# Attention projections as 512-column products handed out block by block inside the attention loop, and the operand copies of the attention issued from ScalarE's queue

## The chip, the cores and the metric

The kernel runs on one core of one Trainium2 chip. Its engines are PE (TensorE, with its weight loads shown apart as PEld), DVE (VectorE), ACT (ScalarE), POOL (GpSimd) and SP (SyncE, which here only issues transfers). The metric is the time of one execution on the device in microseconds; what counts is the median of several runs.

## The reference: one inference step of a two-layer trunk

Rows are 640 tokens of 1024 values: 512 of a new prompt and 8 running streams with 16 new tokens each. Layer 0 mixes with a gated MLP and a short convolution, layer 1 with attention over 16 heads of 64 with a learned decay, and each is followed by a convolutional feed-forward block. The change lies in the attention layer:

```python
def _fox_project(x, w_in, b_f, q_norm, k_norm):
    z = x @ w_in                                  # 1024 -> q, k, v of 1024 each, f of 16
    q, k, v, f = jnp.split(z, [D_C, 2 * D_C, 3 * D_C], axis=-1)
    q = _rmsnorm(q.reshape(b, t, C_HEADS, C_HEAD_DIM), q_norm)
    k = _rmsnorm(k.reshape(b, t, C_HEADS, C_HEAD_DIM), k_norm)
    ...
def _fox_attend(q, k, v, dq, dk, q_pos, k_pos):
    s = jnp.einsum('bthd,bshd->bhts', q, k) * (C_HEAD_DIM ** -0.5)
    s = s + dq - dk                               # cumulated log forget values
    s = jnp.where(k_pos <= q_pos, s, NEG_INF)
    return jnp.einsum('bhts,bshd->bthd', jax.nn.softmax(s), v)
```

The prompt attends to itself; the streams attend to a cache of 256 rows and to their own new rows. The result goes through the output projection `w_out` and is added to the residual. k, v, the forget values and the convolution states are outputs too.

## The kernel before

Every large product is made of three single-pass products of split values (high part times high, low times high, high times low), so a weight tile of 128x1024 is loaded as `raw` (512 KB, from SP), its high part `whi` is cast on ACT, and its low part `wlo` is `raw - whi`. `weights` (L83) makes the low part on DVE (L95); `weights_added` (L107) makes it as a negated copy on ACT (L103) and a transfer from POOL that adds the source on top (L104). There are five `whi`/`wlo` buffers and four of `raw`.

The instructions of each engine run in one fixed order. It is made when the program is built, by a scheduler that follows a model of the time: of the instructions that are ready, it takes the one that was written first. So the place of a call in the Python text is its priority, and what is written late fills the holes of what is written early.

The attention layer (from L935) works on four groups of four heads. For each group `project` (L678) computes q, k and v, 256 columns each: for every one of the five row blocks `tb` of 128 tokens (the fifth holds the streams) 24 products into half a PSUM bank `pj` (L701), eight row chunks `kc` of the weights times three. An eviction on ACT scales them into `z` (L704). For q and k, ACT squares (L709), DVE sums by head (L710) and scales (L300), POOL takes the power -1/2 (L301), and after the fifth row block DVE multiplies the whole tile by the result (L713), and k by its norm as well (L715). `decay` (L607, called after the first q) computes the forget values with 48 products `pf`, a scan, and a way through HBM: `s_b`, `s_d` and `s_n` are written and read back by SP.

Then the group's attention runs. `stream_operands` (L791) transposes the streams' q and k. `operands` (L723) transposes q and k of one pair of heads, and for each of the two heads makes four operand tiles `qa`, `ka`, `qb`, `kb`: two casts on ACT (L738, L741), two on DVE (L740, L743), and four transfers from SP (L739, L742, L745, L746). The four tiles have three buffers each. For each of two pairs a fixed list is walked: `"b30", "s0", "b31", "o", "b20", "s1", "b21", "b10", "b11", "b00", "b01"`. `b31` is the prompt's query block 3 of the pair's head 1, `s0` is a pair of streams, `o` makes the next pair's operands. `prompt_block` (L757) makes two score products (L763, L764), a softmax on DVE and ACT, transposes of the probabilities (L770), a copy (L773 or L775) and the products with v (L777, on a tile of 64 columns of weights). A score needs one of two PSUM banks `sc`.

After the four groups come the eight blocks `po` of the output projection over the first heads (L968 to L979), with products of 320 columns; what needs the last heads follows with the next stage (L993). By the priority above, the projections of group g+1 are what fills PE's holes in the attention of group g, and the blocks `po` fill those of group 3. When nothing of the attention is ready, PE takes one product of 256 columns, then looks again.

The change touches `weights_added`, `project`, `operands`, `prompt_block`, some buffer counts in `stream_operands` and `streams_pair`, the attention part of `build`, and the layout of the weights on the host.

## Time and profile before

| what | value |
|---|---|
| median of 3 runs (1505.16 to 1507.6) | 1505.55 us |
| the profiled execution, its whole time | 1503.4 us |
| its span, from the first instruction to the last | 1501.6 us |
| mean granted TensorE clock | 0.991 |
| HBM read, written | 147.43 MB, 11.54 MB |

The profile is of one execution. Its page gives busy time by engine, the span in 40 slices, the DMA queues, the chain of work that ended last and the costliest groups of instructions. On PE the duration of a matmul is longer than its turn, since matmuls overlap in the pipeline: the time that one takes out of PE's stream is the distance between the starts of neighbours, and the chain in order of time shows it, since there a run of matmuls is listed with the time to the next piece. "LDWEIGHTS" rows (PEld) run beside the matmuls. A row of the queue of an engine (SPq, ACTq) is an instruction that issues a transfer.

### The profile page before, as it was taken

To read this page: it belongs to the slowest core of one execution; us is meant where nothing else is said; L and a number is where in the kernel's file an instruction comes from. 1 tells how busy PE (TensorE), PEld (TensorE's weight loads), DVE (VectorE), ACT (ScalarE), POOL (GpSimd) and SP (SyncE) were. 2 spreads that over 40 slices of the span, in tenths; PEclk is the share of its full clock that TensorE was granted. 3 is DMA by queue.
4 is the path that set the end of the run, shared out by engine and by line. 5 is a ranking of instruction groups with operands and counts; after the bars stand their busy time and mean duration, and the time that the engine had idled before them with its cause. 6 is when DMAs were issued, how large, how long until landed. Compare 5 with 4: busy or idle time off the path is not lost.

```text
span 1501.6 us, 26356 instructions
## 1 busy us (share of the span) xinstructions
PE 1470.4 (98%) x10576; PEld 1417.9 (94%) x10576; DVE 1050.5 (70%) x1799; ACT 727.0 (48%) x1316; POOL 194.5 (13%) x229
## 2 busy tenths in 40 slices
PE   8999999899999999999999999999989999999998
PEld 6999999899999999999989888888979999999998
DVE  6555538977777777576676767768796776777764
ACT  5422325555555555445545454535455554555551
POOL 5100021201100010043111111003210000100000
PEclk9999999899999999999999999999989999999999
DMA  7222213444444444243534343522334433444432
GB/s 272 79 71 72 71 43 88 117 99 117 113 116 113 115 100 111 75 169 106 185 127 139 110 131 106 154 77 88 69 106 119 123 102 97 102 114 113 113 87 85
DMA packets 71786, 164.91 MB, mean 110 GB/s; under 512 B 13600, under 2 KB 21712, under 8 KB 71536
## 3 DMA queue, kind: packets, MB, share of 16 engines
q1 hardware_dynamic: 48304, 133.79, 28.2%
q0 software_dynamic: 10656, 22.02, 9.2%
q10 hardware_dynamic: 12704, 7.41, 1.7%
q8 instruction: 83, 1.36, 0.4%
q14 instruction: 39, 0.32, 0.1%
HBM read 147.43 MB, written 11.54 MB: 106 GB/s over the span
## 4 chain that ended last, share of the span: by engine, by line
PE 88%; DVE 6%; DMA 2%; ACT 2%; issue 2%; SPq 0%; ACTq 0%; DVEq 0%
PE mm L250 36%; PE zx L200 19%; PE pj L701 12%; PE aux L200 8%; PE pv L777 3%; PE po L250 3%; DMA wlo<-w_dn 2%; PE pt L770 1%; DVE hl L281 1%; DVE wlo L95 1%; PE mm L388 1%; PE pt L856 1%; PE sc L763 1%; PE sc L764 1%; DVE sl L136 1%
## 5 line engine op out<-in xcount | busy, mean ns | idle before, releaser
L135 ACT CAST sh<-raw 128x1024 fp32r<-128x1024 f32 (+2 forms) x152 | 142.8, 943 | 135.7 <-PE zx L200 87.0
L136 DVE TENSOR_TENSOR sl<-raw,sh 128x1024 fp32r<-128x1024 f32 (+2 forms) x152 | 165.0, 1092 | 55.4 <-ACT sh L135 55.2
L250 PE MATMUL mm<-sh,wlo 128*128 128x320 f32 x864 | 197.8, 310 | 3.2 <-DMA wlo<-w_dn 2.6
L250 PE MATMUL mm<-sh,whi 128*128 128x320 f32 x864 | 196.6, 310 | 0.6 <-ACT sh L135 0.6
L250 PE MATMUL mm<-sl,whi 128*128 128x320 f32 x864 | 197.0, 309 | 0.0
L200 PE MATMUL zx<-hl,sh 128*128 128x320 f32 x576 | 179.0, 311 | 2.1 <-DVE hl L136 2.0
L200 PE MATMUL zx<-hh,sh 128*128 128x320 f32 x576 | 178.0, 309 | 1.9 <-ACT sn L215 1.9
L200 PE MATMUL zx<-hh,sl 128*128 128x320 f32 x576 | 174.9, 309 | 0.0
L347 DVE SCALAR_TENSOR_TENSOR t<-zp,cst,t 128x656 f32<-128x656 f32 x184 | 163.8, 897 | 11.4 <-ACT t L345 10.3
L94 ACT CAST whi<-raw 128x1024 fp32r<-128x1024 f32 (+3 forms) x96 | 85.8, 896 | 148.9 <-PE mm L250 81.6
L250 PEld LDWEIGHTS mm<-sh,wlo 128*128 128x128 f32 x864 | 143.6, 188 | 5.9 <-DMA wlo<-w_dn 2.8
L358 DVE TENSOR_TENSOR x<-mm,x 128x640 f32<-128x640 f32 x103 | 84.5, 820 | 90.7 <-PE mm L250 90.4
L250 PEld LDWEIGHTS mm<-sh,whi 128*128 128x128 f32 x864 | 144.2, 188 | 1.9 <-ACT sh L135 1.1
L250 PEld LDWEIGHTS mm<-sl,whi 128*128 128x128 f32 x864 | 144.7, 188 | 0.2 <-DVE sl L136 0.2
L701 PE MATMUL pj<-whi,hl 128*128 128x256 f32 x480 | 137.9, 287 | 2.8 <-DVE hl L281 2.8
L701 PE MATMUL pj<-wlo,hh 128*128 128x256 f32 x480 | 137.6, 287 | 0.0
L701 PE MATMUL pj<-whi,hh 128*128 128x256 f32 x480 | 137.3, 287 | 0.0
L95 DVE TENSOR_TENSOR wlo<-raw,whi 128x1024 fp32r<-128x1024 f32 (+3 forms) x96 | 107.9, 1127 | 34.3 <-ACT whi L94 33.7
L250 PE MATMUL mm<-hl,whi 128*128 128x320 f32 x512 | 117.4, 310 | 2.0 <-DVE hl L281 2.0
L250 PE MATMUL mm<-hh,wlo 128*128 128x320 f32 x512 | 117.4, 311 | 0.4 <-DMA wlo<-w_up 0.4
L250 PE MATMUL mm<-hh,whi 128*128 128x320 f32 x512 | 117.7, 311 | 0.0
L200 PEld LDWEIGHTS zx<-hl,sh 128*128 128x128 f32 x576 | 108.4, 188 | 4.1 <-DVE hl L136 3.9
(232 smaller groups left out, 3341.5 us busy)
## 6 DMA issues: line engine op xcount, KB each, us to landing
raw<-w_up SPq DMA_DIRECT2D x88, 512.0 KB
raw<-w_dn SPq DMA_DIRECT2D x36, 512.0 KB
wlo<-w_dn POOLq DMA_DIRECT2D x36, 512.0 KB, 5.9
raw<-w_c SPq DMA_DIRECT2D x24, 512.0 KB
raw<-w_ab SPq DMA_DIRECT2D x16, 512.0 KB
ck<-c_k SPq DMA_DIRECT2D x16, 512.0 KB
cv<-c_v SPq DMA_DIRECT2D x16, 512.0 KB
o_kv<-z ACTq DMA_DIRECT2D x8, 640.0 KB
```

The source lines that it names most:

```text
L94: nc.scalar.copy(out=hi[:, c], in_=raw[:, c])
L95: nc.vector.tensor_tensor(out=lo[:, c], in0=raw[:, c], in1=hi[:, c].bitcast(F32), op=ALU.subtract)
L135: nc.scalar.copy(out=hi, in_=src)
L136: nc.vector.tensor_tensor(out=lo, in0=src, in1=hi.bitcast(F32), op=ALU.subtract)
L200: nc.tensor.matmul(out, lhsT=l[:, c], rhs=r, start=start and p == 0 and i == 0, stop=p == 3 and i == 2, skip_group_check=True)
L250: nc.tensor.matmul(outs[h], lhsT=l, rhs=r[:, h * HT:(h + 1) * HT], start=start and k == 0, stop=stop and k == 2)
L281: nc.vector.scalar_tensor_tensor(out=lo, in0=x, scalar=gs, in1=hi.bitcast(F32), op0=ALU.mult, op1=ALU.subtract)
L347: nc.vector.scalar_tensor_tensor(out=cv[:, 0:CW], in0=zp[:, i:i + CW], scalar=w[:, i:i + 1], in1=cv[:, 0:CW], op0=ALU.mult, op1=ALU.add)
L358: self.nc.vector.tensor_tensor(out=x, in0=ps[:, C0:C0 + T], in1=x, op=ALU.add)
L388: nc.tensor.matmul(pvs[tb], lhsT=l[:, tb * P:(tb + 1) * P], rhs=r[:, (kc % 2) * 512:(kc % 2 + 1) * 512], start=kc == 0 and k == 0, stop=kc ...
L701: nc.tensor.matmul(out[tb], lhsT=l[:, tb * P:(tb + 1) * P], rhs=r[:, c:c + 256], start=kc == 0 and i == 0, stop=kc == 7 and i == 2)
L777: nc.tensor.matmul(ov[64 * hh:64 * hh + 64, i * P:n], lhsT=z[2][:, j, (2 * pair + hh) * 64:(2 * pair + hh) * 64 + 64], rhs=u[:, j * P:(j + ...
```

## The change

`project` is replaced by two functions that return their output tiles and a list of five steps (three for the first call), one for each row block, to be called later. `project_qk` makes q and k of a group together, 512 columns wide; `project_v` makes v of two groups together, 512 wide. A step holds 24 products. The first step of a list loads its four weight tiles; for all but the first lists the first of the four is made with `weights_added`. The norm of q and k is finished in the last step of a list.

q and k of group 0, then `decay`, then v of groups 0 and 1 are done ahead of the attention. The other 20 steps (q and k of groups 1 and 2, v of groups 2 and 3, q and k of group 3) wait in a queue, and so do the eight output blocks in group 3. After chosen blocks of the list one step is taken from the queue; `issue_after` puts its instructions on PE behind the second score product of that block. The table `share` says how many for each group and pair, `after` which blocks. Since a step is now written behind its block, it comes ahead of the later blocks in priority. The output blocks take their weights from `weights_added`.

The four transfers of `operands` go from SP's queue to ACT's, in the loop over both heads. Buffers: the q/k tiles are 512 wide with two buffers (before: 256 wide, three), v has three (two), `sq` is 512 wide with one (256, two), `kts` and `on` one (two), `ckv` two (three).

```diff
-    def weights_added(self, src):
-        raw = self.raw()
+    def weights_added(self, src, cols=1024):
+        raw = self.raw()[:, 0:cols]
         self.nc.sync.dma_start(out=raw, in_=src)
-        return self.added(self.wp, ("whi", "wlo"), raw, src, 1024, 1024)
+        return self.added(self.wp, ("whi", "wlo"), raw, src, 1024, cols)
...
-    def project(self, g, h, first, after_q=None):
+    def walk(self, us, h, tbs, evict):
+        k, nc = self.k, self.nc
+        out = [self.pj.tile([P, 512], F32, tag="pj", name=k.nm("pj")) for _ in tbs]
+        for kc in range(8):
+            wh, wl = us[kc // 2]
+            hh, hl = h[kc]
+            c = (kc % 2) * 512
+            for tb, o in zip(tbs, out):
+                for i, (l, r) in enumerate(((hh, wh), (hl, wh), (hh, wl))):
+                    nc.tensor.matmul(o, lhsT=l[:, tb * P:(tb + 1) * P], rhs=r[:, c:c + 512],
+                                     start=kc == 0 and i == 0, stop=kc == 7 and i == 2)
+        for tb, o in zip(tbs, out):
+            evict(tb, o)
+
+    def project_qk(self, g, h, pairs=False):
...
+        zt = self.zp.tile([P, 5, 512], F32, tag="qk", name=k.nm("z"), bufs=2)
+        ss = self.zp.tile([P, 40], F32, tag="ss", name=k.nm("ss"))
+        def evict(tb, o):
+            nc.scalar.activation(out=zt[:, tb, :], in_=o, func=AF.Copy, scale=self.rt[:, tb:tb + 1])
+            sq = self.zp.tile([P, 512], F32, tag="sq", name=k.nm("sq"), bufs=1)
+            nc.scalar.activation(out=sq, in_=zt[:, tb, :], func=AF.Square)
+            s = ss[:, tb * 8:tb * 8 + 8]
+            nc.vector.reduce_sum(out=s, in_=sq.rearrange("p (h d) -> p h d", d=64), axis=AX.X)
+            k.rstd_of(s, s, 1.0 / 64)
+            if tb < 4:
+                return
+            zh = zt.rearrange("p t (h d) -> p (t h) d", d=64)
+            nc.vector.tensor_tensor(out=zh, in0=zh, in1=ss.unsqueeze(2).broadcast_to([P, 40, 64]), op=ALU.mult)
+            zk = zt[:, :, 256:512].rearrange("p t (h d) -> p t h d", d=64)
+            nc.vector.tensor_tensor(out=zk, in0=zk, in1=..., op=ALU.mult)
+            nc.scalar.dma_start(out=io["o_kv"][0, :, :, 256 * g:256 * g + 256]..., in_=zt[:, :, 256:512])
+        us = []
+        def step(tbs):
+            if not us:
+                us.extend((k.weights_added if g and u == 0 else k.weights)(io["w_qk"][g, u]) for u in range(4))
+            self.walk(us, h, tbs, evict)
+        walk = [(0, 1), (2, 3), (4,)] if pairs else [(tb,) for tb in range(5)]
+        return (zt[:, :, 0:256], zt[:, :, 256:512]), [lambda tbs=tbs: step(tbs) for tbs in walk]
+
+    def project_v(self, gg, h):
...
+        def evict(tb, o):
+            for i, zt in enumerate(zs):
+                nc.scalar.activation(out=zt[:, tb, :], in_=o[:, 256 * i:256 * i + 256], func=AF.Copy, scale=self.rt[:, tb:tb + 1])
...
@@ operands
-            nc.sync.dma_start(out=f(qa[b]), in_=f(qa[a]))
+            nc.scalar.dma_start(out=f(qa[b]), in_=f(qa[a]))
...
-            nc.sync.dma_start(out=f(kb[0:64]), in_=f(ka[a]))
+            nc.scalar.dma_start(out=f(kb[0:64]), in_=f(ka[a]))
...
-            nc.sync.dma_start(out=f(qb[64:68]), in_=io["s_b"][hd, 0:4])
-            nc.sync.dma_start(out=f(kb[64:68]), in_=io["s_b"][hd, 4:8])
+            nc.scalar.dma_start(out=f(qb[64:68]), in_=io["s_b"][hd, 0:4])
+            nc.scalar.dma_start(out=f(kb[64:68]), in_=io["s_b"][hd, 4:8])
@@ build
+    def out_block(ob):
+        n = cut[ob]
+        w = k.weights_added(io["w_oc"][ob, :, 0:n * P], n * P)
...
+    qk, steps = at.project_qk(0, h, True)
+    for f in steps:
+        f()
+    decay()
+    v, steps = at.project_v(0, h)
+    for f in steps:
+        f()
+
+    share = {(0, 0): 3, (0, 1): 4, (1, 0): 4, (1, 1): 4, (2, 0): 3, (2, 1): 2, (3, 0): 4, (3, 1): 4}
+    after = {2: ("b30", "b21"), 3: ("b30", "b31", "b21"), 4: ("b30", "b31", "b21", "b11")}
...
     for g in range(4):
-        z = at.project(g, h, g == 0, decay if g == 0 else None)
-        if g == 3:
+        z = qk + (v[g],)
+        if g == 0:
+            for i in (1, 2):
+                qks[i], steps = at.project_qk(i, h)
+                queue += steps
+            vs, steps = at.project_v(1, h)
+            v += vs
+            queue += steps
+        elif g == 1:
+            qks[3], steps = at.project_qk(3, h)
+            queue += steps
+        elif g == 3:
             o = [k.split(k.hp, HT_, at.o[c]) for c in range(6)]
+            queue += [lambda ob=ob: out_block(ob) for ob in (6, 7, 0, 1, 2, 3, 4, 5)]
...
-                    at.prompt_block(g, pair, int(st[2]), int(st[1]), z)
+                    score = at.prompt_block(g, pair, int(st[2]), int(st[1]), z)
+                    if st in after[share[g, pair]]:
+                        with tc.issue_after(score.ins):
+                            queue.pop(0)()
             at.prompt_end(g, pair)
...
+        qk = qks.get(g + 1)
```

91 lines of the change are left out of this document (35 added, 56 removed).

## The prediction

> **What bounds the kernel now.** I read the page first, then windows over the attention layer, then the chain in order of time for the turn of each kind of matmul. From the page:
>
> ```profile
> span 1501.6 us, 26356 instructions
> ...
> PE 1470.4 (98%) x10576; PEld 1417.9 (94%) x10576; DVE 1050.5 (70%) x1799; ACT 727.0 (48%) x1316; POOL 194.5 (13%) x229
> ...
> PE 88%; DVE 6%; DMA 2%; ACT 2%; issue 2%; SPq 0%; ACTq 0%; DVEq 0%
> ```
>
> PE bounds it: 88% of the chain that ended last. The windows show whether that also holds where the change is (columns: length, then busy time of PE, PEld, DVE, ACT, POOL, granted clock, DMA share, GB/s):
>
> ```profile
> 660.00:676.00 16.00, 13.18 (x103) 12.44 (x102) 12.16 (x17) 3.85 (x5) 7.23 (x12) 1.00 0.49 162
> 676.00:726.00 50.00, 50.00 (x411) 49.86 (x409) 29.80 (x55) 30.44 (x56) 12.99 (x13) 1.00 0.47 150
> 726.00:1016.00 290.00, 290.00 (x2630) 254.31 (x2629) 200.73 (x577) 134.84 (x351) 30.54 (x33) 1.00 0.39 123
> ```
>
> The first projection (660 to 726) leaves PE 2.8 us idle, the attention (726 to 1016) none. DVE is at 69% and ACT at 46% there, so neither binds over the whole stretch. A fuller PE can therefore bring nothing in the attention; only less work on PE can, and any hole that the new order leaves is a loss. How much of the 290 us is what, in counts, with the turns from the chain in order of time (start, time to the next piece, what):
>
> ```profile
> L701 PE MATMUL pj<-wlo,hh 128*128 128x256 f32 x337 | 97.2, 288 | 0.0
> L701 PE MATMUL pj<-whi,hl 128*128 128x256 f32 x336 | 97.0, 289 | 0.0
> L250 PE MATMUL po<-sl,whi 128*128 128x320 f32 x84 | 25.5, 317 | 0.0
> ```
>
> ```profile
> 702.17 14.39 PE pj L701 x120
> 31.83 2.72 PE mm L388 x12
> 1061.75 28.17 PE mm L250 x192
> ```
>
> The turn of a product of 256 columns is 14.39/120 = 0.120 us, of 320 columns 28.17/192 = 0.147, of 512 columns (in the first mixer, same kind of operands) 2.72/12 = 0.227. The 290 us hold 1009 projection products (337 + 2 x 336, the third kind has 336 too), 121 us, and 252 of `po` (3 x 84), 37 us. The other 132 us, 16.5 per pair of heads, are the attention's own.
>
> **The change, part by part.** *512 columns.* 1440 products of 0.120 (172.8 us) become 720 of 0.227 (163.4): 9.4 us less. The Trainium skill, "TensorE: Matmul & The Clock Gate", section "Wait — 56ns, not 53.3ns?", knows only some 2.5 ns beside the columns of a matmul; by that, 720 fewer would save 1.8 us. The three rows above speak for more: 64 columns from 256 to 320 cost 27 ns and 192 from 320 to 512 cost 80, so 0.42 ns each, and 0.120 less 256 of them leaves 13 ns per matmul. I take the rows.
>
> *Ahead of the attention.* The first score now comes at 725.94:
>
> ```profile
> 717.43 8.51 PE pj L701 x71
> 725.94 0.23 PE sc L763
> ...
> 684.16 2.06 PE pf L250 x14
> 686.22 1.11 PE pt L323 x10
> ```
>
> ```profile
> 714.77 0.25 SPq L745 DMA_DIRECT2D qb<-s_b  x1
> ```
>
> By then 431 projection products are done (1440 less 1009; of them the 120 and the 71 above), 51.7 us. After it, 240 of 512 columns must be, 54.4 us: that is 49 products of 256 more. With the 48 `pf` (7.1), the two small groups at L308 and L323 (about 2.3) and 12 transposes (1.3) I get 65.1 us from PE's start at 659.8, so 724.9. But the forget values are also needed: from the end of `pf` (686.2) to the first read of `s_b` (714.8) it takes 28.6 us. `pf` now stands behind all 120 products of q and k, in holes of their evictions or at their end: at about 696 instead of 686. That puts the read at 724.5 and the first score at about 727, 1.2 us later than now and with 5.9 us of projection (49 x 0.120) more behind it. Bounds: 0 later if `pf` goes into holes, 5 later if it comes whole behind q and k.
>
> *The fill of the attention.* 1009 products (121.1 us) become 20 steps of 24, 108.8 us: 12.3 us less between first score and end, the 5.9 and 6.4 from the width. Each pair has 16.5 us of its own and 3, 4, 4, 4, 3, 2 steps of 5.4, so 33, 38, 38, 38, 33 and 27 us; the last two have 120 and 132 products of `po`, 34 and 36. The steps come ahead of later blocks, so in the pairs with three or four PE has something to do until the last short blocks, and those are followed by the next pair's first score. I take 0.5 us of holes there in all (bounds 0 and 6).
>
> *A wait that is new.* In the last pair of group 2 only two steps are left, behind `b30` and `b21`, and the second ends q and k of group 3. Now `po` covers that place; then nothing may, since the output blocks stand behind the first score of group 3. From the end of that step to that score the path is one eviction, square, sum, scale, power, two multiplications, transposes, casts, a transfer. Rows for 256 columns, then the sum for 512 (L783), and PE's rows:
>
> ```profile
> L704 ACT ACTIVATE z<-pj,rt 128x256 f32<-128x256 f32 x43 | 18.6, 472 | 9.0 <-PE pj L701 8.7
> L709 ACT ACTIVATE sq<-z 128x256 f32<-128x256 f32 x28 | 11.2, 419 | 0.0
> L301 POOL TENSOR_TENSOR ss<-ss,mhalf 128x4 f32<-128x4 f32 x30 | 31.1, 1043 | 184.7 <-DVE ss L300 177.9 <-DVE l L786 6.6
> L783 DVE TENSOR_REDUCE m<-sc 128x1 f32<-128x512 f32 x12 | 8.2, 687 | 0.1
> L713 DVE TENSOR_TENSOR z<-z,ss 128x1280 f32<-128x1280 f32 x6 | 8.9, 1485 | 0.4 <-POOL ss L301 0.2
> L715 DVE TENSOR_TENSOR z<-z,atcst 128x1280 f32<-128x1280 f32 x3 | 4.5, 1489 | 0.0
> ```
>
> ```profile
> 732.79 0.44 PE pt L770 x4
> ...
> 785.04 0.80 PE pv L777 x6
> 785.84 0.37 PE pt L770 x2
> ```
>
> ```profile
> 873.10 0.98 PE L731 MATMUL pt<-cst,z 128*128 128x128 f32 x7
> ```
>
> ```profile
> 879.55 0.40 PE L763 MATMUL sc<-ka,qa 128*128 128x512 f32 x1
> ```
>
> Eviction and square of twice the columns I put at 0.7 and 0.65, the sum at 0.7, scale and power at 1.2, the multiplications at 2.9 and 1.5: 7.6 us, and 1 us for the handing on between engines, an estimate. From the transposes to the score 873.10 to 879.55 is 6.5, and the streams' transposes ahead add 0.5. Together 15.6 us. What PE has in that time: four short blocks (score 0.24, transposes 0.11 or 0.37, products with v 0.3 to 0.4 each: about 3.3), the transposes (1.3), and what `b20`, `s1` and `b21` left: from the score at 725.94 to its transposes at 732.79 lie 6.9 us, longer than the step of 5.4, so theirs come behind it, about 4. The hole is 15.6 - 8.6 = 7.0 us. Bounds: 0, if the step comes early; 13, if what is left is done within the step and the six splits of `o` (L951, now ready at the same moment) stand in DVE's way.
>
> *Transfers from ACT.* 64 issues move:
>
> ```profile
> 741.30 0.47 SPq L739 DMA_DIRECT2D qa<-qa  x1
> 745.87 0.47 SPq L742 DMA_DIRECT2D kb<-ka  x1
> 750.91 0.27 SPq L745 DMA_DIRECT2D qb<-s_b  x1
> ```
>
> ```profile
> 871.44 0.35 ACT L803 ACTIVATE qbd<-pt,qn 64x128 f32<-64x128 f32 x1
> 871.58 0.38 ACTq L717 DMA_DIRECT2D o_kv<-z  x1
> 871.81 1.11 ACT L803 ACTIVATE qbd<-pt,qn 64x128 f32<-64x128 f32 x3
> ```
>
> On SP the 9.6 us from the first to the third are waits of an ordered queue, with weight and cache loads behind them; that goes. On ACT an issue of 0.38 us ran beside computing: L803 started again 0.23 us into it. A head's four issues are some 1.5 us. I take 0: ACT is 46% busy, the wait for a free buffer is one that its casts have already. If an issue did wait, the pair's exponentials would stand behind it on ACT, and PE's transposes behind those. Exposed at every head it would be 16 x 1.5 = 24 us of ACT's time, on PE's path only where fill lacks: by my count 3.5 us, 1.0 for two issues in the hole above and 0.3 at the end of each of eight pairs.
>
> *The rest at nothing.* Twelve weight tiles change their DVE split for a transfer that adds:
>
> ```profile
> wlo<-w_dn POOLq DMA_DIRECT2D x36, 512.0 KB, 5.9
> ```
>
> Its 5.9 us are hidden as long as the fifth weight buffer lets one tile be made ahead; without cover each costs up to 5.9 less a step's 5.4. One buffer pair fewer for the caches costs nothing while the streams' two uses lie half a pair apart, over 13 us. The end of the last pair loses nothing: the last output block stands behind `b11`, which is where `po` ends now.
>
> **The sum.** 1.2 - 12.3 + 0.5 + 7.0 = -3.6 us. Against the profiled execution of 1503.4 us (span 1501.6, 1.8 around it) that is 1499.8. The median of the runs is 2.15 higher, so 1505.55 - 3.6 = **1502.0**. A measurement of this kernel can tell about 0.2%, 3 us, from no change.
>
> **The rivals.** *The hole decides* (slower). If the wait for q and k of group 3 is 13 us, PE stands still long enough for its clock to fall. The profile has such a place:
>
> ```profile
> 282.52 0.63 PE L200 MATMUL aux<-sh,sl 128*128 128x320 f32 x1 [2.65 <-DVE sl L136]
> ...
> 270.00:290.00 20.00, 15.12 (x72) 13.53 (x71) 19.96 (x29) 12.91 (x21) 5.57 (x3) 0.74 0.43 138
> ```
>
> There the granted clock is 0.74 of full over 20 us: up to 5.2 us, I take half. (The same page of the Trainium skill, section "What's actually happening", has the clock halved after an idle window of some 3.4 us; by that rule the hole alone would do it, and the row, with a wait of 2.65 us in it, doesn't speak against it.) With the first score 3 late: 3 - 12.3 + 0.5 + 13 + 2.6 = +6.8, 1512.3. For it: that no other work may stand there. It decides from a hole of 10.6 us on, all else as forecast. *No hole*: the step is early enough, or what is left covers it; 1.2 - 12.3 + 0.5 + 1 = -9.6, 1496.0. *ACT's issues or thin fill cost 3.5 more*: 1505.5. *The width brings nothing* (the change doesn't do what it says): a product of 512 among the attention's takes two turns of 256, 0.240; then the 9.4 us are missing, +5.8, 1511.4. The row of 12 at L388 speaks against it, and so does the score of 512 columns at 725.94 with 0.23. (The 2.5 ns of the Trainium skill, above, would come close to this rival.)
>
> **How the numbers follow.** Forecast 0.35, own range 1499 to 1504.5, of which 0.25 is faster and 0.10 within 0.2%. No hole 0.20, faster. ACT or thin fill 0.12, of which 0.10 within and 0.02 slower. The hole 0.28 and the width 0.05, slower. Together faster 0.45, within 0.2% 0.20, slower 0.35. The range goes from no hole to the hole's price, 1496 to 1512.5.
>
> **What would show it.** 720 products, in the place of those of L701, with a turn of 0.227; the first score within 0 to 3 us of 725.9; PE busy throughout the attention but for one hole ahead of group 3's first score, of about 7 us, ended by DVE or ACT; ACT's softmax steps not waiting on its own issues. Wrong would be: holes at every pair's end, a clock below 1.00 in the attention, or a turn of 512 columns near 0.238.

## The result, and the profile after

The changed kernel took 1555.01 us (median of 4 runs, 1550.68 to 1557.42) against 1505.99 for the kernel before on the same chip (1505.16 to 1507.6): a ratio of 1.0322, with a 95% interval of 1.0306 to 1.0338. It is slower by about 49 us. The forecast was 1502.0, and the top of its range 1512.5.

The profiled execution took 1550.68 us, the shortest of the four. Its page has these lines in the places of those shown of before:

```profile
span 1548.9 us, 24813 instructions
...
PE 1476.2 (95%) x9856; PEld 1384.4 (89%) x9856; DVE 1036.2 (67%) x1743; ACT 734.5 (47%) x1288; POOL 200.0 (13%) x221
...
PE 37%; DVE 5%; DMA 1%; ACT 1%; issue 1%; POOL 0%; ACTq 0%; DVEq 0%
```

720 matmuls fewer, and yet PE is busy 6 us longer (why, follows below); its share of the span went from 98% to 95%. (The shares of the chain now add up to 45% of the span: it was followed back only part of the way, so I don't read them.) The windows over the same three stretches as before, with the same columns:

```profile
660.00:676.00 16.00, 14.29 (x71) 11.65 (x70) 11.67 (x14) 4.29 (x7) 7.17 (x9) 1.00 0.50 162
676.00:726.00 50.00, 50.00 (x242) 42.59 (x241) 26.04 (x37) 25.78 (x38) 11.73 (x12) 1.00 0.37 115
726.00:1016.00 290.00, 251.81 (x1726) 191.50 (x1725) 165.53 (x460) 132.11 (x300) 34.60 (x25) 0.91 0.46 132
```

Up to 726 us nothing is lost. Then 290 us that were full have 38 us of idle PE and a granted clock of 0.91. The windows from group to group show it better. Each starts at the first score of a group; the first row is the work ahead of it, and the last ends with the last product with v. First the kernel before, then the changed one:

```profile
659.80:725.90 66.10, 63.28 (x514) 62.49 (x512) 42.16 (x71) 34.22 (x61) 20.32 (x25) 1.00 0.47 153
725.90:802.30 76.40, 76.40 (x712) 67.84 (x711) 52.21 (x150) 37.98 (x98) 9.69 (x11) 1.00 0.43 137
802.30:879.50 77.20, 77.20 (x704) 67.69 (x703) 51.44 (x147) 37.76 (x97) 9.95 (x10) 1.00 0.38 121
879.50:958.90 79.40, 79.40 (x719) 70.50 (x718) 58.43 (x162) 40.22 (x102) 10.82 (x10) 1.00 0.43 131
958.90:1023.10 64.20, 63.44 (x543) 52.88 (x541) 42.55 (x136) 21.34 (x64) 0.64 (x6) 1.00 0.29 86
```

```profile
660.60:741.50 80.90, 65.97 (x322) 55.46 (x320) 42.02 (x56) 37.15 (x56) 19.22 (x21) 0.95 0.51 157
741.50:823.30 81.80, 76.07 (x520) 57.40 (x521) 47.50 (x138) 36.94 (x86) 12.92 (x8) 0.96 0.35 103
823.30:913.40 90.10, 82.75 (x545) 62.72 (x545) 52.10 (x137) 40.24 (x93) 6.99 (x5) 0.94 0.44 130
913.40:993.60 80.20, 68.31 (x473) 50.51 (x473) 47.82 (x138) 37.98 (x89) 11.97 (x9) 0.88 0.48 132
993.60:1073.20 79.60, 75.92 (x605) 65.02 (x605) 42.94 (x139) 26.85 (x70) 3.30 (x9) 0.94 0.34 89
```

I call the sum of five such rows the **stretch**: 363.3 us before, 412.6 after. That difference, 49.3 us, is the whole loss; what lies behind the stretch took 478.5 us before and 475.7 after (span less the end of the stretch). All five parts got longer, each by 0.8 to 15.4 us, so it is not one place. (For one kernel below, x_ops_first, there is no stretch: its trace is of an execution of 3086.85 us, twice as long as its other runs.)

Idle PE is 3.6 us of the stretch before and 43.6 after, so 40.0 of the 49.3 us are idle time. In the other 9.3 PE is busy, and the clock says why. In the trace after, it is at half in seven pieces of the stretch, from 733.6 to 747.2, 822.3 to 829.2, 863.3 to 866.7, 911.1 to 917.9, 948.6 to 952.0, 982.8 to 999.8 and 1030.6 to 1034.0. Together they are 54.6 us, and PE is busy in 36.5 of them; in the stretch before there is no such piece. An estimate from this: work at half clock takes twice its time (a product of 512 columns has a turn of 0.43 us there instead of 0.23, see f_fill below), so some 18 us of PE's work are the price of the clock. Without it the work would be 350.8 us, against 359.7 before: 9 us less, about what the width was to save. So the loss is 40.0 of idle time and 18 of slower work, less 9.

The largest idle pieces, from the order of time of PE (start, duration of the matmul, what, and in brackets the idle time before it with what ended it):

```profile
741.53 0.77 PE L782 MATMUL sc<-ka,qa 128*128 128x512 f32 x1 [13.26 <-DMA qa<-qa]
...
823.33 0.77 PE L782 MATMUL sc<-ka,qa 128*128 128x512 f32 x1 [3.19 <-DMA qa<-qa]
...
913.39 0.77 PE L782 MATMUL sc<-ka,qa 128*128 128x512 f32 x1 [4.68 <-DMA qa<-qa]
...
986.59 0.66 PE L816 MATMUL pt<-cst,z 128*128 128x128 f32 x2 [2.79 <-DVE z L709]
...
993.57 0.79 PE L782 MATMUL sc<-ka,qa 128*128 128x512 f32 x1 [3.39 <-DVE ka L762]
```

They stand at the first score of every group. Three end with the copy of `qa` (a transfer of `operands`), and the two at group 3 with the chain that was forecast. They make 27 of the 43.6 us; the rest is in pieces of under 2 us inside the pairs.

Why the first one is so long shows in PE's and ACT's order of time around it. PE:

```profile
726.80 0.60 PE L816 MATMUL pt<-cst,z 128*128 128x128 f32 x4
727.24 1.04 PE L750 MATMUL pt<-cst,z 128*128 128x128 f32 x8
741.53 0.77 PE L782 MATMUL sc<-ka,qa 128*128 128x512 f32 x1 [13.26 <-DMA qa<-qa]
```

ACT and its queue:

```profile
728.45 0.67 ACT L757 ACTIVATE qa<-pt,qn 64x512 fp32r<-64x512 f32 x1
...
729.45 0.41 ACTq L731 DMA_DIRECT2D o_kv<-z  x1
...
729.96 0.48 ACTq L731 DMA_DIRECT2D o_kv<-z  x1
...
730.54 1.62 ACTq L758 DMA_DIRECT2D qa<-qa  x1
...
741.13 1.28 ACT L805 ACT_TABLE_LOAD   x1 [7.20 <-DMA o_kv<-z]
```

q and k of group 0 have long been ready, but their transposes (L816, L750) come at 726.8, right behind v's last product, because `operands` of group 0 is written behind v. (The last multiplication of k, L711, ended at 711.1.) From there to the score runs a chain of transposes, casts and a copy, with two stores of v (640 KB each) issued just ahead of that copy. And nothing may stand beside it: every step is bound to a score of group 0, the first of them to the very score that waits. Before, that place was covered. The transposes of group 0 ended there with

```profile
717.05 0.38 PE L731 MATMUL pt<-cst,z 128*128 128x128 f32 x2
```

and `717.43 8.51 PE pj L701 x71`, quoted in the prediction, is projection work that PE did while the same chain ran.

### The profile page after: what moved, and what is told of

Same layout as the page of the kernel before. It is cut to its first block, busy times and chain, and to the rows that moved or that the text cites. A ratio compares the mean times of both kernels' runs of the same rounds, so it can differ in the third digit from the quotient of the medians.

```text
span 1548.9 us, 24813 instructions
## 1 busy us (share of the span) xinstructions
PE 1476.2 (95%) x9856; PEld 1384.4 (89%) x9856; DVE 1036.2 (67%) x1743; ACT 734.5 (47%) x1288; POOL 200.0 (13%) x221
## 3 DMA queue, kind: packets, MB, share of 16 engines
q0 software_dynamic: 12384, 26.87, 10.7%
## 5 line engine op out<-in xcount | busy, mean ns | idle before, releaser
L94 ACT CAST whi<-raw 128x1024 fp32r<-128x1024 f32 (+3 forms) x84 | 75.3, 903 | 146.9 <-PE mm L250 81.6
L95 DVE TENSOR_TENSOR wlo<-raw,whi 128x1024 fp32r<-128x1024 f32 (+3 forms) x84 | 96.0, 1148 | 26.1 <-ACT whi L94 25.8
L200 PEld LDWEIGHTS zx<-hh,sh 128*128 128x128 f32 x576 | 108.7, 189 | 2.4 <-ACT sn L215 2.4
L200 PEld LDWEIGHTS zx<-hh,sl 128*128 128x128 f32 x576 | 107.7, 188 | 0.0
L688 PE MATMUL pj<-whi,hl 128*128 128x512 f32 x240 | 95.9, 400 | 1.7 <-DVE hl L281 1.7
```

Of the source, the lines that this page charges most:

```text
L94: nc.scalar.copy(out=hi[:, c], in_=raw[:, c])
L95: nc.vector.tensor_tensor(out=lo[:, c], in0=raw[:, c], in1=hi[:, c].bitcast(F32), op=ALU.subtract)
L200: nc.tensor.matmul(out, lhsT=l[:, c], rhs=r, start=start and p == 0 and i == 0, stop=p == 3 and i == 2, skip_group_check=True)
L688: nc.tensor.matmul(o, lhsT=l[:, tb * P:(tb + 1) * P], rhs=r[:, c:c + 512], start=kc == 0 and i == 0, stop=kc == 7 and i == 2)
```

## The experiments

Sixteen kernels were run. What I compare is the stretch, which is read from one trace to a few tenths, and the ratio of the whole time. In all of them the part behind the stretch has the same text, but it wasn't always equally long; that is told at the end of this section. Each stretch is from one execution. How far such figures scatter shows in that part behind: in after, a_head1_act, x_ops_ahead, x_ahead_sp and y_cover PE does the same sequence of work there, and it took 474.8 to 479.2 us. So I take differences of 4 us and less between two stretches as not told apart. All numbers first; PE busy, idle PE, the busy time at half clock and the mean clock are those of the stretch:

| label | edit | stretch | PE busy | at half clock | idle | clock | ratio of whole time (95%) |
|---|---|---|---|---|---|---|---|
| before | | 363.3 | 359.7 | 0 | 3.6 | 1.00 | 1 |
| after | | 412.6 | 369.0 | 36.5 | 43.6 | 0.93 | 1.0322 (1.0306 to 1.0338) |
| a_ops_sp | after, operand transfers on SP | 406.5 | 367.1 | 31.2 | 39.4 | 0.94 | 1.0266 (1.0244 to 1.0288) |
| a_kv_sp | after, k/v stores on SP | 407.1 | 367.2 | 29.4 | 39.9 | 0.95 | 1.0322 (1.0299 to 1.0344) |
| a_head1_act | after, head 0's transfers on SP | 413.0 | 371.6 | 41.1 | 41.5 | 0.93 | 1.0319 (1.0299 to 1.034) |
| b_ops_act | before, operand transfers on ACT | 369.2 | 362.6 | 3.4 | 6.6 | 1.00 | 1.0084 (1.0061 to 1.0106) |
| x_ops_first | after, group 0's operands ahead of v | | | | | | 1.029 (1.0257 to 1.0324) |
| x_ops_ahead | after, every group's operands ahead | 393.7 | 363.6 | 23.3 | 30.1 | 0.96 | 1.0189 (1.0172 to 1.0205) |
| x_unlock | after, no bond | 377.9 | 358.9 | 14.7 | 19.0 | 0.98 | 1.0109 (1.0091 to 1.0126) |
| w_only | 512 columns, not dealt, SP | 379.9 | 362.8 | 22.2 | 17.1 | 0.97 | 1.01 (1.0085 to 1.0115) |
| f_fill | after, products nobody reads in the first hole | 413.4 | 378.9 | 31.0 | 34.5 | 0.95 | 1.0385 (1.036 to 1.0411) |
| d_256 | after, products of 256 columns | 459.9 | 395.7 | 73.8 | 64.2 | 0.89 | 1.0677 (1.0654 to 1.0699) |
| x_ahead_sp | operands ahead, on SP | 388.6 | 362.7 | 22.1 | 25.9 | 0.96 | 1.0139 (1.0122 to 1.0157) |
| x_ahead_sp_free | the same, no bond | 369.7 | 356.7 | 9.6 | 13.0 | 0.99 | 1.006 (1.004 to 1.0079) |
| q_256 | the same, products of 256 columns | 372.8 | 367.4 | 9.4 | 5.4 | 0.99 | 1.0108 (1.009 to 1.0126) |
| z_g2 | x_ahead_sp, other shares | 385.1 | 360.6 | 15.6 | 24.5 | 0.97 | 1.0103 (1.008 to 1.0125) |
| y_cover | steps bound to their pair only | 384.7 | 360.0 | 19.8 | 24.7 | 0.97 | 1.0131 (1.0112 to 1.015) |
| y_cover_free | the same, no bond | 376.9 | 359.4 | 15.4 | 17.5 | 0.98 | 1.0075 (1.0049 to 1.0101) |

PE busy less half of the time at half clock, an estimate of the work at full clock, is 350 to 353 us in every kernel with 512 columns (f_fill less the 12.3 us of its unread products) and 359 to 363 in the four with 256 (before, b_ops_act, d_256, q_256). So the work hardly differs within a width; idle time and clock make the kernels differ.

**Whose transfers delay the first score?** Three kernels move transfers of the changed kernel, and one moves those of the kernel before.

```diff
 a_ops_sp: all four transfers of operands
-            nc.scalar.dma_start(out=f(qa[b]), in_=f(qa[a]))
+            nc.sync.dma_start(out=f(qa[b]), in_=f(qa[a]))
 a_kv_sp: both stores of k and v
-            nc.scalar.dma_start(out=io["o_kv"]...
+            nc.sync.dma_start(out=io["o_kv"]...
 a_head1_act: in operands
+            q = nc.scalar if hh else nc.sync
-            nc.scalar.dma_start(out=f(qa[b]), in_=f(qa[a]))
+            q.dma_start(out=f(qa[b]), in_=f(qa[a]))
 b_ops_act: before, all four transfers of operands
-            nc.sync.dma_start(out=f(qa[b]), in_=f(qa[a]))
+            nc.scalar.dma_start(out=f(qa[b]), in_=f(qa[a]))
```

> The changed kernel with the four operand transfers of both heads issued from SP again. Queue theory (the copies stood behind the stores of k and v, 640 KB each in pieces of 1 KB, in ACT's row of the transfer engines): the three waits for qa of 13.3, 4.7 and 3.2 us go and with them most of three low stretches of the clock (13.7, 6.8, 6.8 us at half), so some 30 us less, about 1525. Dealing theory (the new order of the projections alone leaves the holes): the waits get another name and the time stays above 1545.

> The changed kernel with the operand transfers left on ACT and the eight stores of k and v issued from SP. Queue theory: as good as with the operand transfers on SP, about 1525, and the first score's wait for qa of 13.3 us gone. Issue theory (ACT is held up by issuing 64 transfers and its softmax steps come late): no better than 1550.

> The changed kernel with the first head's operand transfers on SP and only the second head's on ACT. Queue theory: the first score (head 0) no longer waits, the second head's b31 waits instead, but a step of 5.4 us of products lies between; about 1530. Issue theory: half of what the transfer of both costs, about 1540.

> The kernel before with the operand transfers of both heads issued from ACT and nothing else changed. Queue theory: at each of the four group starts the copies stand behind one store of k or v (640 KB, half of the changed kernel's two at the first), 2 to 5 us each on a PE that has projection products only if the order put them there, so 1510 to 1525. Dealing theory: within 3 us of 1506.

With the operands back on SP the first hole is still there:

```profile
738.38 0.76 PE L782 MATMUL sc<-ka,qa 128*128 128x512 f32 x1 [10.88 <-DMA qa<-qa]
```

It went from 13.26 to 10.88 us, and the stretch by 6.1. With the stores on SP instead, the hole is shorter still:

```profile
736.84 0.76 PE L782 MATMUL sc<-ka,qa 128*128 128x512 f32 x1 [8.24 <-DMA qa<-qa]
```

and the stretch went by 5.5, though the whole time didn't (1.0322). With head 0 on SP alone the hole is 10.63 us and the stretch no shorter; I have no account of that. In the kernel before, moving the transfers to ACT costs 5.9 in the stretch and 1518.27 us in all, as the queue theory had it. So copies and stores in one row of ACT are worth 5 to 6 us of the stretch, in both kernels, but the theory that the transfers make the loss falls: the three came to 1545.76, 1553.41 and 1553.51 us where it had 1525 to 1530, and over 40 of the 49 us stay. Nor is it ACT held up by its issues: PE's waits that end with ACT are 2.5 us in the whole attention of the changed kernel. Why 8 to 11 us of the hole stay wherever the copy or the stores are issued, no run shows by itself. The window of the changed kernel from 726 us to the score shows what the copy stands among:

```profile
726.00:741.50 15.50, 2.27 (x17) 1.83 (x15) 4.91 (x7) 7.42 (x14) 0.92 (x1) 0.74 0.97 285
```

The DMA engines are busy at 0.97 with 285 GB/s: the two stores of v and the weight transfers of the next steps (`raw<-w_qk`, `raw<-w_vc`, `wlo<-w_qk`, 512 KB each) all start when v ends.

**Are the operands written too late?** In x_ops_first the operands of group 0 are written ahead of v, in x_ops_ahead also those of each later group, behind `b21` of the pair before.

```diff
+    ahead = lambda g, z: (at.stream_operands(g, z), at.streams_start(g), at.operands(g, 0, z))
+    nxt = ahead(0, qk)
     v, steps = at.project_v(0, h)
...
-        sops = at.stream_operands(g, z)
-        at.streams_start(g)
+        sops, _, ops = nxt
...
+                    if st == "b21" and pair == 1 and g < 3:
+                        nxt = ahead(g + 1, qks[g + 1])
```

> The changed kernel, but the operands of group 0 (and its stream operands and cache loads) are written ahead of the steps of v; nothing else. Theory 'written behind v': the hole of 13.3 us at the first score is bare because the transposes of group 0 come behind v's last product; ahead of v they are covered by v's 120 products, the hole and the low clock of 13.7 us behind it go, and the time falls by 15 to 20 us, to about 1537. Theory 'transfers': the hole stays over 8 us, since the copies wait behind the stores on ACT's row, and the time stays within 5 us of 1553. Theory 'dealing as such': the hole goes, but the time falls by less than 8 us, because a later hole takes it up.

> The changed kernel with the operands of every group ahead: group 0's ahead of v, those of group g+1 behind pair 1's block b21 of group g. If the holes at all first scores come from operands written too late, those of 3.2 and 4.7 us go with the one of 13.3, and the time is 1525 to 1535, at least 4 us below the kernel with group 0's alone. If they come from the last projection step that ends just before, they stay, and the two times are within 3 us.

The first score of x_ops_ahead, in the order of time of PE:

```profile
728.46 0.39 PE L688 MATMUL pj<-wlo,hh 128*128 128x512 f32 x1
728.68 0.39 PE L782 MATMUL sc<-ka,qa 128*128 128x512 f32 x1
...
805.03 0.47 PE L782 MATMUL sc<-ka,qa 128*128 128x512 f32 x1 [0.92 <-DVE p L808]
...
966.31 0.66 PE L816 MATMUL pt<-cst,z 128*128 128x128 f32 x2 [7.84 <-DVE z L709]
```

It comes at 728.7 without a hole, 12.9 us earlier, and that of group 1 waits 0.9 us, where it waited 3.2. The stretch falls by 18.9 us (18.0 between a_ops_sp and x_ahead_sp, where the same edit is made with the transfers on SP), the ratio by 0.0133, some 20 us: more than the 12.9 of the one place, as expected if all groups' operands are late. What stays is group 3's wait, now in one piece of 7.84 us at the transposes. The 1532.71 us of x_ops_ahead lie in the band for operands written too late (1525 to 1535). The kernel with group 0's alone gained about 5 us instead of 15 to 20, by the time alone the band of 'dealing as such'; where the rest of its first hole went stays open.

**What does the clock cost?** 54 products of 512 columns that nothing reads stand in the first hole, behind the transposes.

```diff
+            if g == 0 and pair == 0:
+                spare = at.pj.tile([P, 512], F32, tag="pj", name=k.nm("fill"))
+                for i in range(54):
+                    nc.tensor.matmul(spare, lhsT=h[0][0][:, 0:P], rhs=h[1][0][:, 0:512], start=True, stop=True)
             at.prompt_start(pops[pair])
```

> The changed kernel with 54 products of 512 columns that nothing reads, between the transposes of group 0's first operands and its first score: about 54 x 0.227 = 12.3 us of work in the hole of 13.3 us. They add no time of their own there, so what changes is the clock behind the hole. Theory 'clock': the half clock of 13.7 us behind it goes, which is 6.9 us, and the time falls by 4 to 8 us. Theory 'only the idle time counts': the time stays within 2 us.

Its window over the hole, and the one from the first score to that of group 1:

```profile
726.00:741.60 15.60, 14.16 (x70) 11.56 (x68) 4.43 (x6) 6.72 (x14) 0.92 (x1) 1.00 0.95 287
...
741.60:823.10 81.50, 74.72 (x521) 56.69 (x521) 48.20 (x139) 37.43 (x86) 12.71 (x8) 0.97 0.35 103
```

The clock in the hole is 1.00 instead of 0.74, and group 0 takes 81.5 us instead of 81.8. The stretch is the same to 0.8 us. (The whole time is longer by some 8 us, which neither theory had; in the two traces that lies behind the stretch, 485.9 us against 475.7.) But the run says little about the clock behind the hole, which was its question. Of the 13.7 us at half clock that the expectation puts behind the hole, 7.9 lie inside it, where PE has nothing to do and loses nothing. 5.7 lie behind the first score, and there the products of the changed kernel have a turn of 0.43 us:

```profile
744.46 0.63 PE L688 MATMUL pj<-whi,hh 128*128 128x512 f32 x1
744.88 0.63 PE L688 MATMUL pj<-whi,hl 128*128 128x512 f32 x1
```

In f_fill the clock is at half there too, only later: from 743.7 to 747.2 us. So the edit gave PE four products, about 1 us, by 747.4, and 0.3 of it is left at the next group's first score. A low clock inside a hole cost nothing here; what the other 18 us of slower work would bring, no run isolates.

**Is it the bond?** x_unlock takes the bond out of the changed kernel; x_ahead_sp has operands ahead and on SP with the bond, x_ahead_sp_free without.

```diff
                     if st in after[share[g, pair]]:
-                        with tc.issue_after(score.ins):
-                            queue.pop(0)()
+                        queue.pop(0)()
```

> The changed kernel without the bond of a step to its score: the steps are written at the same places, but the scheduler may put them ahead of that score. Theory 'lock': what should fill the holes is held behind the score that makes them, so the idle time of PE in the attention falls from 44 us to under 15 and the time to 1505 to 1520. Theory 'priority': the steps would be placed as before even so, because of where they are written; the time stays over 1540.

> The changed kernel with the operands of every group written ahead and all operand transfers on SP again. The operands ahead brought 21 us, SP 8 to 9 us. If the two are separate causes: 1522 to 1527. If SP's gain came from the same chain ahead of the first scores: 1530 to 1535.

> As the kernel with operands ahead and SP, but the steps are not bound to their scores. Theory 'late operands plus bond': with both gone nothing is left but the width, 1494 to 1500. Theory 'thin fill': unbound steps are used up early, as in the two unbound kernels, where they ended at 894 us; groups 2 and 3 stay thin, the holes of 2 to 3 us and the half clock behind them stay, and the time is 1505 to 1515.

Without the bond the changed kernel's stretch falls by 34.7 us, to 377.9: the operands are still late, and the first score comes even later, but unbound steps cover them:

```profile
743.39 0.39 PE L688 MATMUL pj<-whi,hh 128*128 128x512 f32 x1
743.62 0.40 PE L782 MATMUL sc<-ka,qa 128*128 128x512 f32 x1
```

That is the largest gain of a single edit. The time, 1520.42 us, is at the upper end of what 'lock' had, and 'priority' (over 1540) falls; idle time is 19.0 us, where 'lock' had under 15. x_ahead_sp came to 1526.78, in the band of two separate causes. Where the operands are in time, the bond is worth 388.6 - 369.7 = 18.9. With both, x_ahead_sp_free is at 1.006 (1515.85 us, just over the band of 'thin fill'; the 1494 to 1500 of the width alone fall), and its groups look like this:

```profile
660.40:731.00 70.60, 68.90 (x335) 58.08 (x335) 41.98 (x56) 35.90 (x55) 18.25 (x20) 1.00 0.42 126
731.00:822.60 91.60, 91.60 (x600) 70.62 (x600) 56.04 (x146) 46.88 (x96) 19.44 (x13) 1.00 0.55 160
822.60:907.50 84.90, 81.23 (x565) 62.09 (x563) 49.51 (x138) 43.44 (x100) 10.16 (x8) 1.00 0.45 132
907.50:960.70 53.20, 48.88 (x418) 36.74 (x418) 41.95 (x127) 26.93 (x73) 4.50 (x4) 0.94 0.64 169
960.70:1030.10 69.40, 66.11 (x547) 54.30 (x547) 44.73 (x143) 24.11 (x71) 1.51 (x7) 0.98 0.34 98
```

Group 0 is full and takes 91.6 us, group 2 takes 53.2 and has 4.3 us of holes: the unbound steps are used up early. Before, the first three groups were even (76.4 to 79.4) and full. That is the thin fill that the expectation names.

**Is the width real?** w_only has 512 columns without dealing: the steps of the next groups are written behind each group's attention, unbound, operands on SP. d_256 splits each product of the changed kernel into two of 256, q_256 does so in x_ahead_sp_free.

```diff
 w_only, on a_ops_sp (called behind each group's attention)
-                    if st in after[share[g, pair]]:
-                        with tc.issue_after(score.ins):
-                            queue.pop(0)()
             at.prompt_end(g, pair)
+        while queue:
+            queue.pop(0)()
 d_256, q_256
-                    nc.tensor.matmul(o, lhsT=l[:, tb * P:(tb + 1) * P], rhs=r[:, c:c + 512], ...
+        for w in (0, 256):
...
+                        nc.tensor.matmul(o[:, w:w + 256], lhsT=l[:, tb * P:(tb + 1) * P], rhs=r[:, c + w:c + w + 256], ...
```

> The 512-wide steps alone: projections of the next groups written behind each group's attention, at the lowest priority and without a bond, output blocks behind group 3, operand transfers from SP. My sum's term of width is 9.4 us for all of them: if it is real and the holes come from the dealing, the time is 1492 to 1499. If the width itself makes holes (24 products of 0.227 us ahead of a waiting score, or steps too coarse), it is 1505 to 1520. If the buffers that were cut (q/k two, ckv two) make them, over 1520.

> The changed kernel with every projection product split into two of 256 columns, as many as before the change: the dealing without the width. By the turns of the trace (0.120 and 0.227 us) PE gets 720 x (0.240 - 0.227) = 9.4 us more. Theory 'the gain of the width reaches the end': 8 to 12 us slower than the changed kernel. Theory 'it is lost in the holes': less than 4 us slower.

> The kernel with operands ahead, transfers on SP and no bond, with every projection product split into two of 256 columns. Theory 'the width is real and reaches the end': PE gets 720 x (0.240 - 0.227) = 9.4 us more and the time is 8 to 14 us over that kernel's 1515.9. Theory 'the width brings nothing at the end': within 4 us of it.

w_only came to 1520.26 us (1.01), on the edge between the band for holes by the width or the steps (1505 to 1520) and that for the buffers that were cut (over 1520), so it doesn't tell these two apart; no run gives the buffers back. Its operands of group 0 are behind v as well, and the first score comes at 741.96. d_256 fitted neither theory: 47 us more in the stretch, where 9.4 were due. Steps and scores follow each other as in the changed kernel, but the small pieces between two scores (transposes, products with v) are ordered otherwise. Idle time is 20.6 us more; seven scores now wait for ACT's softmax, 14.2 us in all. PE busy is 26.7 us more, and by the estimate under the table 18.6 of these are the clock, which is at half in 73.8 us of PE's work instead of 36.5; some 8 are left for the width. So its whole time is no measure of the width. q_256 against x_ahead_sp_free, two kernels without bonds, does. The stretch of x_ahead_sp_free:

```profile
660.40:1030.10 369.70, 356.73 (x2462) 281.83 (x2461) 234.20 (x608) 177.26 (x392) 53.87 (x52) 0.99 0.48 137
```

and of q_256:

```profile
659.40:1032.20 372.80, 367.41 (x3182) 327.41 (x3181) 234.76 (x608) 176.61 (x392) 54.05 (x52) 0.99 0.45 136
```

The narrow products cost PE 10.7 us of work (forecast 9.4), but the stretch is only 3.1 us longer, which is within the scatter: idle time falls from 13.0 to 5.4. Where holes are left, most of the saved products turn into holes. (The whole time differs by 6.9 us, between the bands of the two theories; in the traces 6.7 us lie behind the stretch.)

**Can the dealing be mended?** z_g2 is x_ahead_sp with 4 and 3 steps in group 2, two of them output blocks, and 3 and 3 in group 3. In y_cover the steps are written behind their pair and bound to its first score only; the next operands come as soon as their q and k are done. y_cover_free has no bond.

```diff
 z_g2, on x_ahead_sp
-    share = {..., (2, 0): 3, (2, 1): 2, (3, 0): 4, (3, 1): 4}
+    share = {..., (2, 0): 4, (2, 1): 3, (3, 0): 3, (3, 1): 3}
...
+            elif g == 2:
+                o = [k.split(k.hp, HT_, at.o[c]) for c in range(4)]
+                queue += [lambda ob=ob: out_block(ob) for ob in (6, 7, 0, 1, 2, 3, 4, 5)]
 y_cover, on z_g2
             at.prompt_end(g, pair)
+            for n in range(share[g, pair]):
+                if pair and g < 3 and n == need[g]:
+                    nxt = ahead(g + 1, qks[g + 1])
+                with tc.issue_after(lead.ins):
+                    queue.pop(0)()
```

> The kernel with operands ahead, transfers on SP and the bond, with group 2's pairs holding 4 and 3 steps: the last of q and k of group 3 right behind the first block of the second pair, then two output blocks there; group 3 keeps six. The hole of 7.7 us ahead of group 3's transposes and the half clock of 17 us around it go. Theory 'group 3's hole costs what I put on it (7 us) and more by the clock': 1526.8 falls by 7 to 14 us, to 1513 to 1520. Theory 'a later hole takes it up': less than 4 us.

> Steps written behind each pair, at lower priority than its blocks, bound only to the pair's first score; output blocks from group 2's second pair on; operands ahead, transfers on SP. So steps fill product by product and are not used up in earlier pairs. Theory 'the bond and thin fill made the rest': idle time of PE in the attention under 12 us and 1495 to 1510. Theory 'the chain of each block bounds the attention': 1515 to 1530 as in the bound kernel.

> The same without any bond: what is written behind a pair may be used earlier, when its data are there. If early use is what thins groups 2 and 3, it is 3 to 15 us slower than the kernel with the bond to the pair; if the bond is what costs, it is faster by as much.

z_g2 is 3.7 us faster than x_ahead_sp by the medians, 5.4 by the ratios, and 3.5 in the stretch. The hole at group 3's transposes is gone, but another has come:

```profile
952.13 1.08 PE L855 MATMUL scs<-ck,qbd 128*32 128x256 f32 x8 [6.29 <-DMA ck<-c_k]
```

a cache tile that comes late. The change left two buffers for these tiles where there were three; whether that is the reason was not tried. y_cover missed its mark too (1.0131): bound to the pair's first score, the steps can't cover the place ahead of that score, and there the largest piece of its 24.7 us of idle time stands:

```profile
901.36 0.77 PE L782 MATMUL sc<-ka,qa 128*128 128x512 f32 x1 [7.35 <-DMA qa<-qa]
```

Without the bond the same kernel is 10.8 us faster. No kernel of these is faster than the one before.

**The part behind the stretch.** It took 475 to 479 us in some kernels and 483 to 490 in others (b_ops_act, a_kv_sp, f_fill, d_256, x_ahead_sp_free, q_256), though its text is the same. The scheduler had put its instructions in another order there: in the six long ones PE's order in the feed-forward block differs from that of the others. Their waits there for low parts of weights, in the changed kernel, f_fill and q_256 in turn (what, total, times, longest):

```profile
PE mm L250 <- DMA wlo<-w_dn: 1.0, 1, 1.0
```

```profile
PE mm L250 <- DMA wlo<-w_dn: 6.2, 5, 2.3
```

```profile
PE mm L250 <- DMA wlo<-w_dn: 9.4, 8, 2.0
```

That the order makes the difference is a reading; no run tests it, and it isn't all: f_fill, d_256 and q_256 have one sequence of PE's work there and took 485.9, 484.6 and 490.0 us. So some 10 us of a whole time can lie far behind the edit, which is why I read the stretch.

## Why the prediction was wrong

The sum was 1.2 - 12.3 + 0.5 + 7.0 = -3.6. By its steps:

- **512 columns** (-9.4 of the -12.3): right as a cost. Two runs of products from the chain of the changed kernel:

```profile
876.31 4.57 PE pj L688 x20
...
898.85 2.97 PE pj L688 x13
```

  are 0.229 and 0.228 us a product, against a turn of 0.227 forecast, and q_256 shows 10.7 us of PE's work. The estimate of the work at full clock agrees: 9 us less than before. Wrong in what it brings: in the pair with the fewest holes only 3.1 of the 10.7 us are left in the stretch (6.9 in the whole time). The argument that less work on PE is gained takes a full PE for granted, and no kernel with 512 columns here has one.
- **Ahead of the attention** (+1.2, first score at 727, bounds 0 to 5): this step failed. The sum got PE to the end of its products rightly (the transposes stand at 726.8, and where the operands are ahead the first score comes at 728.7), but it left out the chain from there to the score. I had read that 71 leftover products stood ahead of the first score, and counted their time; I didn't ask what they covered, nor where the operands are written against v, and that every step which could cover them now is bound behind the score. Measured: 741.5, so 14.5 us.
- **The fill of the attention** (0.5 us of holes, bounds 0 and 6): this step failed most. I gave group 0 33 + 38 = 71 us and group 1 76; they took 81.8 and 90.1, of which PE was busy 76.1 and 82.8. At full clock that would be some 73 and 78 (5.7 and 9.2 us of it are at half clock), so the pairs' sums were right as work to about 2 us. But they took for granted that a step fills whatever hole comes. A bound step can't: it comes as 24 products right behind one score, and the holes ahead of the next group's first score, and behind the last step of a pair, stay open. Idle time in the groups, without group 3's hole, is 22 us; undoing the bond gives 34.7 us back in the changed kernel, and 18.9 once the operands are in time.
- **The clock** (not in the sum): a term that was missing. The sum priced PE's work at the turns of a full clock, and a clock below 1.00 in the attention stood only among the signs of being wrong. With the holes came 54.6 us at half clock, 36.5 of them in PE's work: some 18 us, by the estimate above.
- **A wait that is new** (7.0 ahead of group 3's first score): right, 6.2 in two pieces. The pieces of 2.79 and 3.39 stand where they were forecast, and end with the chain named. Of the holes at the four groups it is the one that I looked for, because there the fill visibly runs out; at the other three the fill was there and couldn't be used.
- **ACT's transfers** (taken as nothing, with a rival of 3.5 us): 5 to 6 us of the stretch, from a_ops_sp, a_kv_sp and b_ops_act. Issues were counted, but not what the copies have ahead of them. The Trainium skill, "DMA: Bandwidth & Descriptors", section "Queues, rings and completion order", says that SP and ACT each have one ring on each of the same 16 DMA engines, and that a completion is written only after every earlier write of that engine, across its queues. The trace agrees so far as it goes: with the copy on SP 10.88 us of hole stay, with the stores on SP 8.24. No run here shows the order of the writes themselves.
- **The rival "the hole decides"** had a hole of 13 us at group 3. One of 13.3 came at group 0; that the figures are alike is chance, for its cause is another. What I added for the clock (2.6 us) is about what half clock behind that one hole makes in PE's work (5.7 us, so 2.9), but f_fill doesn't show whether it would come back at the end. The Trainium skill, "TensorE: Matmul & The Clock Gate", section "What's actually happening", has the clock halved after an idle window; the trace agrees for this hole (0.74 over it, 1.00 with the unread products). Why the clock fell for 3.4 us in f_fill all the same, behind only 1.44 us of idle time, no run shows.

How the 49.3 us of the stretch come together, each from a pair of kernels: operands on SP 6.1 (412.6 to 406.5), operands written ahead 17.9 (to 388.6), the bond 18.9 (to 369.7), and 6.4 that stay against 363.3. The order of the edits matters. With the operands ahead first it is 18.9, then 5.1 for SP; with the bond first it is 34.7 for the bond, and only 8.2 are left for the other two together (377.9 to 369.7). Late operands and the bond share most of their loss, since an operand that is late costs only where nothing may cover it.

In the last 6.4, PE is idle 9.4 us more and busy 3.0 less (its work some 8 less by the estimate, of which half clock takes 4.8 back). The first row of those windows is 4.5 us longer than before (70.6 against 66.1), but holds 5.6 more of work, v of group 1, which is missing later. The holes stand in groups 1, 2 and 3 (3.7, 4.3 and 3.3 us), where the fill is thin. What the buffers that were cut have to do with that wasn't tried, and a dealing that avoids it was not found.

## What to carry to other kernels

Before fill work is moved or bound, list what it covers now, place by place: at each wait of the bottleneck engine that the profile doesn't show, ask which chain would show if the work beside it were gone. Work that is bound behind an instruction can't cover the wait of that instruction, so the chain ahead of it must be written ahead of the last free work. A saving on a full engine is a saving only while it stays full; with holes left, most of it turned into more hole here. And a hole on PE may cost more than its length, by the estimate here 18 us beside 40: look at the clock behind it, and at the turn of the products there.

## What the runs showed of the hardware

- A small copy between partitions (128 KB) took some 11 us when it started together with large transfers: issued at 730.54 us, waited for until 741.53, with the DMA engines busy at 0.97 (285 GB/s). Changing its queue from ACT to SP took 2.4 us off the hole, changing that of the stores ahead of it 5.0; starting the copy ahead of them took off all of it.
- The granted clock was at half from 733.6 us, some 5 us into a hole of 13.3 us, to 747.2, 5.7 us behind its end, and 54 products that nothing reads kept it at 1.00 over the hole, but not behind it. In the stretches of all these traces it was at half in pieces of 3.41 us and multiples of it (6.82, 10.24, 13.65, 17.07, 23.89).
- At half clock a product of 512 columns had a turn of 0.43 us instead of 0.23. PE's busy time less half of that at half clock came to 350 to 353 us in every kernel with 512 columns, while the busy time itself went from 356.7 to 371.6 (f_fill left out of both).
- The same part of the program took 475.7 us behind the stretch with 1.0 us of waits for `wlo<-w_dn`, and 490.0 with 9.4; which of the rest comes from the order of its instructions is open.
